# Two heads' scores on the row halves of TensorE, and values with scores in one run per block

## The chip, the cores and the metric

The kernel runs on one core of a Trainium2 chip. The metric is the device time of one execution in microseconds (us), lower is better. The engines are named as in the profile: PE (TensorE's products) and PEld (its weight loads), DVE (VectorE), ACT (ScalarE), POOL (GpSimd) and SP (SyncE, here only a queue of transfers).

## The reference

One layer of a decoder with three parallel groups of heads, for a new sequence of 4096 positions (the prompt) and for 8 x 8 single positions against a cache (the sample batch). Width 1024.

```python
def _layer(x, conv_buf, buf_k, buf_v, mem_k, mem_v, g_pre, g_post, w_in, conv_w, sink, w_out, prompt):
    h = _rmsnorm(x, g_pre)
    z = h @ w_in
    cb, cc, ch, cg, q, k, v, ag, mq, mg = _split_cols(z)
    u = cc * ch
    up = jnp.concatenate([conv_buf, u], axis=1)
    conv = conv_w[0] * up[:, 0:t] + conv_w[1] * up[:, 1:t + 1] + conv_w[2] * up[:, 2:t + 2]
    out_a = jax.nn.silu(cg) * cb * conv
    ...
    o_b = _window_prompt(q, k, v, sink_g)        # 8 heads of 64, 2 kv heads, window 128, one sink logit per head
    out_b = jax.nn.silu(ag) * o_b
    o_c = _mem_attend(mq.reshape(n, t, MEM_HEADS, HEAD_DIM), mem_k, mem_v)   # 4 heads of 64, 256 memory tokens
    out_c = jax.nn.silu(mg) * o_c
    y = jnp.concatenate([out_a, out_b, out_c], axis=-1) @ w_out
    return x + _rmsnorm(y, g_post), new_conv, new_k, new_v
```

Everything is float32. The softmax of the window takes the sink logit into its sum and its maximum. Outputs are y for prompt and sample batch and the new caches.

## The kernel before, in words

The first part, to about 952 us, is the input projection (products `c`, line L359). It leaves queries, keys, values and gates in DRAM (`qd`, `vd`, `md`). In its last third `third_jobs` weaves in the attention of chunk 0 and the scores of group 2.

The second part is the attention of the rest with the output projection. The prompt has 16 chunks of 256 positions (`CT`), each of two groups of 128 queries, so 32 groups; output block b is the 128 rows of group b. The blocks run in the order 0 to 30, 32 (the sample batch), 31. `Block.run` makes a block in two halves `y_0` and `y_1` of 512 columns, each 24 products of 128 x 512 (L1434): 8 steps k, and for each three products of high and low parts (`mh`, `ml`, which `split` makes on ACT and DVE). After each half DVE multiplies by the norm's weight into `yn` (L1441) and ACT squares with a row sum (L1442). After `y_1` DVE adds the sums (`yst`, L1447), POOL raises them to the power -1/2 (L1448), and DVE makes the residual sum `xr` (L1452), which is stored.

`events_of(i)` hangs the attention of later groups into block i, at (p, k): half p, ahead of step k. From block 2 on these are: at (0,4) `group_run`, the values of group i+2 with their gates (L1099, L1155) and the transposes of group i+3 (L1197, L1126); at (0,6), (1,0), (1,2) and (1,4) the four pieces of the scores of group i+4; at (1,0) also the split of block i+1. Loads of later chunks and the sample batch's stages hang in the same way. A scheduler orders each engine's instructions from this program; the engines then work through their orders.

A group's scores take eight window heads (`ws`, L1175) and four cross heads (`xs`, L1112). Queries lie with their high part on one half of the 128 rows and their low part on the other. Keys lie twice, with high parts (then low parts) on both halves, so two products of 128 rows and 256 columns per head sum all four combinations of parts. A piece of window scores is emptied from PSUM by an ACT copy of the own block's half (L1177) and a DVE copy_predicated of the earlier half (L1178), after which maximum, exps and scaling work in SBUF on four heads at a time. Cross scores are read from PSUM by maximum and exp. The transposed window weights are masked on POOL into `wpv` and `wpt` (L1204, L1207).

PSUM in this part has four banks in rotation for scores and transposes (tag `s`), two for y (tag `z`), and two for values (`pv`).

Of the kernel before, what the change touches and what calls it, by code (L numbers as in the profile page):

```python
# [51 lines left out]
def hybrid_layer(ctx: ExitStack, tc: tile.TileContext, a: dict):  # L52
# [664 lines left out]
    def third_start():  # L717
        keep = right.enter_context(tc.tile_pool(name="memkv", bufs=1, side="right"))
        third["mk"] = keep.tile([P, 2, 4, 256], F32R, name="mk")
# [64 lines left out]
    def mem_keys():  # L784
        mk, keys = third["mk"], third.pop("keys")
        t = third["ps"].tile([P, 512], F32, tag="m", name="mkt").rearrange("p (j m k) -> p j m k", j=2, m=2)
        for m in range(2):
            for j in range(2):
                TE.transpose(t[:, j, m, :], keys[:, m, j * P : (j + 1) * P], ident)
        for hh in range(2):  # L790
            src = t[hh * 64 : hh * 64 + 64].rearrange("p j m k -> p j (m k)")
            hi = mk[hh * 64 : hh * 64 + 64, 0, hh:4:2, :]
            for half in (hh, 1 - hh):
                r = slice(half * 64, half * 64 + 64)
                S.copy(mk[r, 0, hh:4:2, :], src)
                V.tensor_tensor(mk[r, 1, hh:4:2, :], src, f(hi), op=ALU.subtract)

    def third_jobs(b, p):
# [19 lines left out]
        if n > 13 and third["chunk"]:  # L818
            jobs.append(third["chunk"].pop(0))
        elif n > 13 and len(chunks) == 1:  # L820
            jobs.append(lambda: chunk_load(1))
        elif n > 13 and early[0] < 4 and n >= 38:
            jobs.append(lambda u=early[0]: scores(2, u))
            early[0] += 1
# [4 lines left out]
    def first_chunk():  # L829

        mem_stack.close()
        third["work"] = right.enter_context(tc.tile_pool(name="work", bufs=5, side="right"))
        chunk_load(0)
        chunk = chunks[0]
        chunk.load_mix()
        third["chunk"] = pieces = [lambda: chunk.values(None)]
        for left, right_, both in chunk.pairs():
            pieces += [lambda u=u: next(u, None) for _ in range(2) for u in (left, right_)] + [both]
# [141 lines left out]
    def open_attention():  # L980

        nonlocal ps, mixp, wp, xp, vp, bp, bq, yp
# [4 lines left out]
        ps = {tag: ctx.enter_context(tc.tile_pool(name=f"ps{tag}", bufs=bufs, space=bass.MemoryType.PSUM))  # L987
              for tag, bufs in (("s", 4), ("z", 2), ("pv", 1))}
        ps["t"] = ps["s"]
# [4 lines left out]
        xp = att.enter_context(tc.tile_pool(name="xp", bufs=2))  # L994
# [3 lines left out]
    ps = mixp = wp = xp = vp = bp = bq = yp = None  # L998
    att = ctx.enter_context(ExitStack())

    def psum(tag, name):
# [7 lines left out]
    def work(pool, shape, tag, name, **kw):  # L1009

        if ps is None or tag in ("sm", "p"):
            return third["work"].tile(shape, F32, tag="u", name=name)
        return pool.tile(shape, F32, tag=tag, name=name, **kw)

    def both_values(o, left, right):

        n = len(left)
        for i in range(n):
            for half, steps in enumerate((left, right)):
                v, p = steps[i]  # L1020
                cs = slice(64 * half, 64 * half + 64)
                TE.matmul(o[cs], v[:, cs], p, start=i == 0, stop=i == n - 1, tile_position=(0, 64 * half))  # L1022

    class Chunk:
# [10 lines left out]
        def load_keys(self):  # L1035
            c, t0 = self.c, self.t0

            self.kst = self.pool().tile([P, 4, P + CT], F32R, tag="k", name=f"kst{c}")
# [7 lines left out]
            self.vT = self.pool().tile([P, CT], F32, tag="vT", name=f"vT{c}")  # L1046
            DMA.dma_start(self.vT, vd[:, self.ts])

        def load_queries(self):

            self.q = self.pool(True).tile([P, 12, CT], F32R, tag="q", name=f"q{self.c}")
            for part in range(2):
                for hh in range(2):
                    half = hh if part == 0 else 1 - hh
                    G.dma_start(self.q[half * 64 : half * 64 + 64, hh::2, :],  # L1055
                                  qd[part, 1:7, hh * 64 : hh * 64 + 64, self.ts].rearrange("j p n -> p j n"))

        def load_mix(self):

            if self.c % 3 == 0:  # L1060
                self.mix = place.rearrange("p a k n -> p (a k n)")[:, : KT * CT].rearrange("p (k n) -> p k n", k=KT)
            else:
                self.mix = (yp if self.c % 3 == 2 else mixp).tile([P, KT, CT], F32, tag="mix", name=f"mix{self.c}", bufs=1)
            DMA.dma_start(self.mix, md[:, :, self.ts].rearrange("k p n -> p k n"))

        def values(self, vt_prev, pv=None):

            self.vts = [vt_prev]
            ts = [psum("t", f"vtp{self.c}_{i}")[:, 0:P] if pv is None else pv[:, 1, 256 + P * i : 256 + P * i + P] for i in range(2)]
# [10 lines left out]
        def pairs(self):  # L1080
            w, x = [self.window_pair(i) for i in range(2)], [self.cross_pair(i) for i in range(2)]
            return [w[0], x[0], w[1], x[1]]

        def group(self, i):

            return Group(self.window_pair(i), self.cross_pair(i))

        def cross_pair(self, j):

            pts = [[], []]  # L1090

            def both(pv=None):
                o = psum("pv", f"xo{self.c}_{j}")[:, :CT] if pv is None else pv[:, 0, 256 : 256 + CT]
                both_values(o, *([(third["mv"][:, kt, j * P : (j + 1) * P], pts[hh][kt]) for kt in range(2)]
                                 for hh in range(2)))

                def gate():
                    g = self.mix[:, 2 + j, :]
                    V.tensor_tensor(g, g, o, op=ALU.mult)  # L1099
                return gate if pv is not None else gate()  # L1100

            return *(self.cross_unit(2 * j + hh, pts[hh]) for hh in range(2)), both

        def cross_unit(self, h, pts):
            c, nb = self.c, CT // P
            q = self.q[:, h]
            p = work(xp, [P, nb, 256], "p", f"xp{c}_{h}")
            mx, nm, den, rd = (tiny.tile([P, 4], F32, tag=n, name=f"x{n}{c}_{h}") for n in ("mx", "nm", "den", "rd"))
            s = psum("s", f"xs{c}_{h}").rearrange("p (b k) -> p b k", b=nb)
            for i in range(nb):  # L1110
                for part in range(2):
                    TE.matmul(s[:, i, :], q[:, i * P : i * P + P], third["mk"][:, part, h, :], start=part == 0, stop=part == 1)  # L1112
            V.tensor_reduce(mx[:, :nb], s, axis=AX.X, op=ALU.max)
            V.tensor_scalar(nm[:, :nb], mx[:, :nb], -SCALE, None, op0=ALU.mult)  # L1114
            for i in range(nb):
                S.activation(p[:, i, :], s[:, i, :], AF.Exp, bias=nm[:, i : i + 1], scale=SCALE, accum_out=den[:, i : i + 1])  # L1116
            V.reciprocal(rd[:, :nb], den[:, :nb])  # L1117
            for i in range(nb):

                G.tensor_scalar(p[:, i, :], p[:, i, :], rd[:, i : i + 1], 0.5, op0=ALU.mult, op1=ALU.mult)  # L1120
            yield 1
            pt = work(xp, [P, 2, CT], "xpt", f"xpt{c}_{h}")
            t = psum("t", f"xt{c}_{h}").rearrange("p (k n) -> p k n", k=2)
            for kt in range(2):
                for i in range(nb):
                    TE.transpose(t[:, kt, i * P : (i + 1) * P], p[:, i, kt * P : (kt + 1) * P], ident)  # L1126
                pts.append(pt[:, kt])
            (S.copy if h % 2 else V.tensor_copy)(pt, t)


        def window_pair(self, i):

            steps = [[], []]

            def both_halves(pv):
                o = pv[:, :, :256].rearrange("p a (h q) -> p a h q", h=4)
                for n in range(2):  # L1140
                    for kvh in range(2):
                        cs = slice(64 * kvh, 64 * kvh + 64)
                        v, p3 = steps[kvh][n]
                        TE.matmul(o[cs, n], v[:, cs], p3[:, :, 64 * n : 64 * n + 64], start=True, stop=False,  # L1144
                                  tile_position=(0, 64 * kvh))
                for n in range(2):
                    for kvh in range(2):
                        cs, rs = slice(64 * kvh, 64 * kvh + 64), slice(64 - 64 * n, 128 - 64 * n)
                        v, p3 = steps[kvh][n]
                        TE.matmul(o[cs, 1 - n], v[rs, cs], p3[rs, :, 64 - 64 * n : 128 - 64 * n], start=False, stop=True,  # L1150
                                  tile_position=(64 - 64 * n, 64 * kvh))

                def gate():
# [477 lines left out]
```

## Time and profile before

| | |
|---|---|
| runs, median (lowest to highest) | 1551.85 us (1550.77 to 1553.34), 3 runs |
| the profiled execution, its own time | 1557.0 us |
| its span | 1555.2 us |
| granted TensorE clock over the span | 0.998 |
| PE busy in the span | 1535.2 us |
| DVE, ACT, POOL busy | 1155.1, 788.9, 377.8 us |

The profile is of one execution, and its times are in microseconds from the start of the span. A row of the timeline has the start, the length, engine, line, operation and tiles; "x8" says how many instructions were put together; brackets at its end tell how long the engine idled before it and what released it. A row of the chain of waits has start, length and the engine and line that the path runs through. A row of a stretch has its ends, its length, the busy time of PE, PEld, DVE, ACT and POOL (with instructions), the granted clock, the DMA share and GB/s.

### The profile page before, as it was taken

Reading aid. Unit: us, or ns where it says so; the run is one execution under the profiler, and the core shown is the slowest. Engines: PE = TensorE matmul, PEld = TensorE weight load, DVE = VectorE, ACT = ScalarE, POOL = GpSimd, SP = SyncE. Lnnn points to the kernel's source line nnn. Section 1 sums busy time; section 2 is a strip of 40 time slices with the busy share of each in tenths; the row PEclk is TensorE's granted clock in tenths of the full one; section 3 lists DMA queues with packets and bytes.
Section 4 is the critical chain, followed back from the end, with each engine's and each line's share of the span. In section 5 each row is a group of like instructions: output and inputs, shape, how many; then the busy total and the mean of one; then the engine's idle time right before and its main releaser. Section 6 shows DMA issues by size and latency. Waiting matters only on the chain.

```text
span 1555.2 us, 30088 instructions
## 1 busy us (share of the span) xinstructions
PE 1535.2 (99%) x11341; PEld 1405.0 (90%) x11341; DVE 1155.1 (74%) x2045; ACT 788.9 (51%) x1999; POOL 377.8 (24%) x602
## 2 busy tenths in 40 slices
PE   9989999999999999999999999999999999999998
PEld 9989999999999999999999998788888788888776
DVE  5769888898988777896687678666666666666653
ACT  6776666475322222344455446555565555565532
POOL 0222333211400000000001202544444444444310
PEclk9999999999999999999999999999999999999999
DMA  9979999878755333569666959986766666666432
GB/s 251 164 239 221 285 287 266 258 240 291 205 178 178 124 116 120 195 207 323 227 221 191 279 211 291 266 164 155 159 147 146 146 158 151 160 148 154 143 125 68
DMA packets 175110, 305.59 MB, mean 196 GB/s; under 512 B 31093, under 2 KB 104821, under 8 KB 174933
## 3 DMA queue, kind: packets, MB, share of 16 engines
q1 hardware_dynamic: 128069, 226.69, 47.3%
q0 software_dynamic: 46176, 75.92, 23.5%
q8 instruction: 90, 1.47, 0.4%
q10 hardware_dynamic: 720, 1.05, 0.2%
q14 instruction: 55, 0.45, 0.1%
HBM read 196.54 MB, written 108.05 MB: 196 GB/s over the span
## 4 chain that ended last, share of the span: by engine, by line
PE 81%; DMA 7%; DVE 5%; issue 3%; ACT 2%; POOL 1%; SPq 0%; ACTq 0%; DVEq 0%; POOLq 0%
PE c L359 42%; PE y L1434 23%; PE ws L1175 4%; PE xs L1112 2%; PE pv L1022 2%; PE wt L1197 2%; PE xt L1126 2%; PE pv L1144 2%; DMA nat<-in_x_p 1%; PE pv L1150 1%; DMA x_0B<-in_xt 1%; DMA x_7T<-hd_T 1%; PE mem_acc L775 1%; DMA vT<-vd 1%; DMA wr_2A<-in_w_in 1%
## 5 line engine op out<-in xcount | busy, mean ns | idle before, releaser
L1434 PE MATMUL y<-wo,mh 128*128 128x512 f32 (+1 forms) x1040 | 347.0, 392 | 0.0
L366 DVE TENSOR_TENSOR z<-c,z 128x520 f32<-128x520 f32 (+1 forms) x308 | 195.0, 645 | 93.9 <-PE c L359 92.7
L1434 PEld LDWEIGHTS y<-wo,mh 128*128 128x128 f32 x1040 | 194.7, 188 | 38.6 <-issue 2.8
L1434 PE MATMUL y<-wo,ml 128*128 128x512 f32 (+1 forms) x520 | 202.2, 389 | 0.0
L1188 ACT ACTIVATE sm<-sm,wnm 128x128 f32<-128x128 f32 x256 | 99.4, 389 | 76.9 <-DVE wnm L1182 76.9
L1120 POOL TENSOR_SCALAR xp<-xp,xrd 128x256 f32<-128x256 f32 x128 | 60.5, 485 | 265.0 <-DVE xrd L1117 265.0
L1434 PEld LDWEIGHTS y<-wo,ml 128*128 128x128 f32 x520 | 97.9, 188 | 14.2
L1177 ACT COPY sm<-ws 128x256 f32<-128x256 f32 x128 | 46.3, 369 | 66.6 <-PE ws L1175 63.3
L1175 PEld LDWEIGHTS ws<-kst,q 128*128 128x128 f32 x512 | 69.3, 191 | 5.8 <-ACT wpt L1199 1.2
L1441 DVE TENSOR_TENSOR yn<-y,gpost 128x512 f32<-128x512 f32 (+1 forms) x66 | 45.1, 683 | 37.6 <-PE y L1434 35.3
L1175 PE MATMUL ws<-kst,q 128*128 128x256 f32 x512 | 71.9, 283 | 0.8 <-ACT wpt L1199 0.8
L1178 DVE COPY_PREDICATED sm<-wmask,ws 128x256 f32<-128x256 uint8 x124 | 54.1, 442 | 18.1 <-ACT sm L1177 16.7
L1207 POOL TENSOR_SCALAR_AFFINE_SELECT wpt<-wpt 128x512 f32<-128x512 f32 x64 | 55.4, 893 | 45.7 <-ACT wpt L1199 45.4
L1452 DVE SCALAR_TENSOR_TENSOR xr<-yn,yst,xr 128x1024 f32<-128x1024 f32 (+2 forms) x34 | 42.7, 1258 | 30.0 <-POOL yst L1448 30.0
L734 POOL MEMSET negs<- 128x1 f32 x1 | 0.1, 98 | 264.6 <-PE c L359 264.6
L1116 ACT ACTIVATE xp<-xs,xnm 128x256 f32<-128x256 f32 x128 | 58.1, 461 | 3.9 <-DVE xnm L1114 3.7
L1055 POOL DMA_DIRECT2D q<-qd x64 | 42.8, 679 | 65.2 <-DMA qd<-zh 49.3
L1199 ACT COPY wpt<-wt 128x512 f32<-128x512 f32 x64 | 34.7, 588 | 44.6 <-PE wt L1197 28.0
L1204 POOL TENSOR_SCALAR_AFFINE_SELECT wpv<-wpt 128x512 f32<-128x512 f32 x62 | 39.6, 669 | 51.5 <-ACT wpt L1199 51.5
L368 ACT COPY z<-c 128x520 f32<-128x520 f32 (+1 forms) x44 | 24.4, 554 | 51.2 <-PE c L359 48.5
L1044 POOL DMA_DIRECT2D kst<-qd x64 | 38.7, 624 | 47.4 <-PE ws L1175 23.8
L1442 ACT ACTIVATE y<-y 128x512 f32<-128x512 f32 (+1 forms) x66 | 38.4, 582 | 22.6 <-DVE yn L1441 22.4
(962 smaller groups left out, 5119.3 us busy)
## 6 DMA issues: line engine op xcount, KB each, us to landing
q<-qd POOLq DMA_DIRECT2D x64, 384.0 KB, 7.6
xr<-in_x_p SPq DMA_DIRECT2D x32, 512.0 KB
nat<-in_x_p SPq DMA_DIRECT2D x39, 416.0 KB
o_yp<-xr SPq DMA_DIRECT2D x31, 512.0 KB
md<-th POOLq DMA_DIRECT2D x48, 260.0 KB, 6.3
qd<-zh SPq DMA_DIRECT2D x48, 260.0 KB
qd<-z SPq DMA_DIRECT2D x48, 260.0 KB
kst<-qd POOLq DMA_DIRECT2D x60, 192.0 KB, 3.6
```

The costliest lines, as they stand in the source:

```text
L359: TE.matmul(bank[:, :HW], l, r, start=first and i == 0, stop=last and i == 3 * KH - 1)
L366: add = lambda dst, other: V.tensor_tensor(dst, c, other, op=ALU.add)
L1055: G.dma_start(self.q[half * 64 : half * 64 + 64, hh::2, :], qd[part, 1:7, hh * 64 : hh * 64 + 64, self.ts].rearrange("j p n -> p j n"))
L1116: S.activation(p[:, i, :], s[:, i, :], AF.Exp, bias=nm[:, i : i + 1], scale=SCALE, accum_out=den[:, i : i + 1])
L1120: G.tensor_scalar(p[:, i, :], p[:, i, :], rd[:, i : i + 1], 0.5, op0=ALU.mult, op1=ALU.mult)
L1175: TE.matmul(s3[:, hh, :], self.q[:, 4 + 2 * (2 * half + hh) + kvh, i * P : i * P + P], self.kst[:, 2 * kvh + part, i * P : i * P + 2 * P], ...
L1177: S.copy(sm[:, 2 * half : 2 * half + 2, :], s3[:, :, P : 2 * P])
L1178: V.copy_predicated(sm[:, 2 * half : 2 * half + 2, :], third["wmask"], third["negs"].unsqueeze(2).to_broadcast([P, 2, P]) if first else s3 ...
L1188: S.activation(sm[:, hh, :], sm[:, hh, :], AF.Exp, bias=nm[:, hh : hh + 1], scale=SCALE, accum_out=den[:, hh : hh + 1])
L1207: G.affine_select(p3, p3, pattern=[[0, 4], [1, P]], compare_op=ALU.is_ge, fill=0.0, base=0, channel_multiplier=-1)
L1434: TE.matmul(acc, self.hl[l][:, k], wo[k][c0 // 512][:, r, c0 % 512 : c0 % 512 + c1 - c0], start=j == 0, stop=j == passes * KT - 1)
L1441: V.tensor_tensor(yn[:m, c0:c1], acc[:m], gpost[:m, c0:c1], op=ALU.mult)
```

## The change

A group's scores now use tiles of 64 rows. Two heads lie on the two row halves of the array, each with its own PSUM bank, and three products per head (high by high, low by high, high by low) take the place of the four combinations. So a group takes 36 products of 64 rows, in 18 pairs. Keys and queries are loaded once and not twice.

Values of group i+1 and then all scores of group i+3 stand at (0,0) of block i in one run, whose products are held in the program's order (`tiled`). The transposes of group i+2 stand at (1,0), the split of block i+1 at (1,3).

PSUM has six single banks b0 to b5 with fixed users, beside `pv`: window scores in 0 to 3, cross scores in 4 and 5, `y_0` in 0, `y_1` in 5, transposes of window weights in 1 and 2, of cross weights in 3 and 4. The window softmax of all eight heads is done at once. The sample batch's stages are hung at other places and banks. Shared work buffers are 3 of 1024 columns instead of 5 smaller ones.

```diff
-        if tag == "pv":
-
-            return ps[tag].tile([P, 2, 512], F32, tag=tag, name=name)[:, 0]
-        return ps[tag].tile([P, 512], F32, tag="s" if tag == "t" else tag, name=name)
+        return ps["b"].tile([P, 512], F32, tag=f"b{bank}", name=name)
...
+    def tiled(o, w, x, **kw):
+
+        ins = TE.matmul(o, w, x, **kw)
+        if run_open[0] and ps is not None:
+            tc.keep_in_program_order(ins)
+        run_open[0] = True
...
-            for kvh in range(2):
-                for half in range(2):
-                    G.dma_start(self.kst[half * 64 : half * 64 + 64, 2 * kvh : 2 * kvh + 2, lo:],
-                                  qd[:, 0, kvh * 64 : kvh * 64 + 64, t0 - P + lo : t0 + CT].rearrange("a p n -> p a n"))
+            G.dma_start(self.kst[:, :, lo:], qd[:, 0, :, t0 - P + lo : t0 + CT].rearrange("a p n -> p a n"))
...
+        def scores(self):
+            self.open_scores(0)
+            self.open_scores(3)
+            bands = [psum(n, f"ws{self.b}_{n}").rearrange("p (h k) -> p h k", h=2) for n in range(4)]
+            cross = [psum(4 + hh, f"xs{self.b}_{hh}").rearrange("p (j k) -> p j k", j=2) for hh in range(2)]
+            self.bands(bands[:2], 0)
+            self.crosses(cross)
+            self.bands(bands[2:], 1)
+            self.band_softmax()
+
+        def both_rows(self, outs, q, k):
+
+            for n, (qp, kp) in enumerate(((0, 0), (1, 0), (0, 1))):
+                for u in range(2):
+                    r = slice(64 * u, 64 * u + 64)
+                    tiled(outs[u], q[r, qp], k[r, kp], start=n == 0, stop=n == 2, tile_position=(64 * u, 0))
...
+        def band_out(self, s3, half, kvh):
+            to = self.sm[:, 4 * kvh + 2 * half : 4 * kvh + 2 * half + 2, :]
+            S.copy(to, s3[:, :, P : 2 * P])
+            V.copy_predicated(to, third["wmask"], third["negs"].unsqueeze(2).to_broadcast([P, 2, P]) if self.b == 0 else s3[:, :, 0:P])
...
+    def values_and_scores(i):
+
+        run_open[0] = False
+        if 2 <= i + 1 < 2 * NCH:
+            groups.pop(i + 1).values()
+        if i + 3 < 2 * NCH:
+            groups[i + 3] = Group(chunks[(i + 3) // 2], (i + 3) % 2)
+            groups[i + 3].scores()
...
-                acc = psum("z", f"y{b}_{p}")[:, : c1 - c0]
+                acc = psum((0, 5, 1)[p], f"y{b}_{p}")[:, : c1 - c0]
...
+        at(0, 0, values_and_scores, i)
         if i + 2 < len(blocks):
-            at(0, 0 if i != 26 else 1, blocks[i + 2].load)
...
-            at(0, 4, group_run, i + 2, i + 3)
-            at(0, 6, scores, i + 4, 0)
-            at(1, 0, scores, i + 4, 1)
-            at(1, 0, split)
-            at(1, 2, scores, i + 4, 2)
-            at(1, 4, scores, i + 4, 3)
+            at(0, 0, blocks[i + 2].load)
...
+        at(1, 0, transposes, i)
+        if i + 1 < len(blocks) and blocks[i + 1].b != 32:
+            at(1, 3, blocks[i + 1].split)
```

More of the change, by code (lines that the diff above doesn't have):

```diff
@@ L789, in mem_keys @@
                 TE.transpose(t[:, j, m, :], keys[:, m, j * P : (j + 1) * P], ident)
[L790 to L796, printed above, removed]
+        src = t.rearrange("p j m k -> p j (m k)")
+        S.copy(mk[:, 0], src)
+        V.tensor_tensor(mk[:, 1], src, f(mk[:, 0]), op=ALU.subtract)
     def third_jobs(b, p):
@@ L831, in first_chunk @@
         mem_stack.close()
-        third["work"] = right.enter_context(tc.tile_pool(name="work", bufs=5, side="right"))
+        third["work"] = right.enter_context(tc.tile_pool(name="work", bufs=3, side="right"))
         chunk_load(0)
         chunk = chunks[0]
+        chunk.load_values()
         chunk.load_mix()
-        third["chunk"] = pieces = [lambda: chunk.values(None)]
-        for left, right_, both in chunk.pairs():
-            pieces += [lambda u=u: next(u, None) for _ in range(2) for u in (left, right_)] + [both]
+        third["chunk"] = [lambda: chunk.values(None)]
+        for i in range(2):
+            pair = Group(chunk, i)
+            third["chunk"] += [lambda pair=pair, n=n, fn=fn: fn(pair, n) for fn, ns in (
+                (Group.early_scores, (0, 1, 2)), (Group.early_transposes, (0, 1)), (Group.early_values, (1,)),
+                (Group.early_scores, (3,)), (Group.early_transposes, (2, 3)), (Group.early_values, (3,))) for n in ns]
     sums_at = {(0, 3 + i): pair for i, pair in enumerate(PHASES[1])}
@@ L1078, in values @@
                 self.vts.append(vt)
[L1080 to L1102, printed above, removed]
@@ L1124, in cross_unit @@
-            for kt in range(2):
[L1125 to L1153, printed above, removed]
-                    g = self.mix[:, 4:8, i * P : i * P + P].rearrange("p h (a q) -> p a h q", a=2)
-                    V.tensor_tensor(g, g, o, op=ALU.mult)
-                return gate
-            def both():
-                o = psum("pv", f"wo{self.c}_{i}")
-                both_values(o, *steps)
-                gate = self.mix[:, 4:8, i * P : i * P + P]
-                V.tensor_tensor(gate, gate, o.rearrange("p (h q) -> p h q", h=4), op=ALU.mult)
-            return *(self.window_unit(i, kvh, steps[kvh]) for kvh in range(2)), both if self.c == 0 else both_halves
@@ L1210, in hybrid_layer, with early_transposes @@
-    class Group:
-        def __init__(self, window, cross):
-            self.units, self.both = [*window[:2], *cross[:2]], (cross[2], window[2])
-        def scores(self, n):
-            next(self.units[n])
-        def transposes(self):
-            for unit in self.units:
-                next(unit, None)
-    groups = {}
-    def scores(g, n):
-        if g < 2 * NCH:
-            if n == 0:
-                groups[g] = chunks[g // 2].group(g % 2)
-            groups[g].scores(n)
-    def group_run(values, transposes):
-        gates, c = (), transposes // 2
-        fresh = transposes % 2 == 0 and c < NCH
-        if values < 2 * NCH or fresh:
-            pv = ps["pv"].tile([P, 2, 512], F32, tag="pv", name=f"pv{transposes}")
-        if 2 <= values < 2 * NCH:
-            gates = [both(pv) for both in groups.pop(values).both]
-        if fresh:
-            chunks[c].values(chunks[c - 1].vts[2], pv)
-        for gate in gates:
-            gate()
-        if transposes < 2 * NCH:
-            groups[transposes].transposes()
+        def early_transposes(self, n):
+            if n == 0:
+                pt = work(f"wpt{self.b}").rearrange("p (u n) -> p u n", u=2)
+                pv = work(f"wpv{self.b}").rearrange("p (u n) -> p u n", u=2) if self.b else None
+                for u in range(2):
+                    self.pt[u], self.pv[u] = pt[:, u], pv[:, u] if self.b else None
+            if n == 2:
+                xpt = work(f"xpt{self.b}").rearrange("p (u n) -> p u n", u=2)
+                for u in range(2):
+                    self.xpt[u] = xpt[:, u]
+            if n < 2:
+                self.band_transposes(n, psum(0, f"wt{self.b}_{n}"))
+            else:
+                self.cross_transposes(n - 2, psum(0, f"xt{self.b}_{n}"))
@@ new lines, in cross_transposes, with cross_values @@
+        def cross_transposes(self, u, t):
+            t3 = t.rearrange("p (k n) -> p k n", k=2)
+            for kt in range(2):
+                for j in range(2):
+                    TE.transpose(t3[:, kt, j * P : (j + 1) * P], self.p[:, u, j, kt * P : (kt + 1) * P], ident)
+            (S.copy if u else V.tensor_copy)(self.xpt[u], t)
+        def cross_values(self, o):
+            c = self.chunk
+            for j in range(2):
+                both_values(o[:, j * P : j * P + P], *([(third["mv"][:, kt, j * P : (j + 1) * P],
+                                                         self.xpt[hh][:, CT * kt + P * j : CT * kt + P * j + P]) for kt in range(2)]
+                                                       for hh in range(2)))
+            g = c.mix[:, 2:4, self.i * P : self.i * P + P]
+            V.tensor_tensor(g, g, o.rearrange("p (j n) -> p j n", j=2), op=ALU.mult)
@@ new lines, in early_values @@
+        def early_values(self, n):
+            c = self.chunk
+            if n == 3:
+                self.cross_values(psum(0, f"xo{self.b}")[:, :CT])
+                return
+            o = psum(0, f"wo{self.b}")
+            both_values(o, *([(v, p[u]) for v, p in zip(c.vts[self.i : self.i + 2], (self.pv, self.pt)) if p[u] is not None]
+                             for u in range(2)))
+            g = c.mix[:, 4:8, self.i * P : self.i * P + P]
+            V.tensor_tensor(g, g, o.rearrange("p (h q) -> p h q", h=4), op=ALU.mult)
@@ L1408, in split @@
             if b == 32:
-                hi = mixp.tile([P, KT, CT], F32R, tag="mix", name="mh_s", bufs=1)[:, :, :P]
+                hi = third["work"].tile([P, KT, P], F32R, tag="u", name="mh_s")
                 S.copy(hi[:, :, 0:NS], mix_s)
@@ L1460, in hybrid_layer @@
     chunk_load(2)
+    chunks[2].load_values()
     blocks[0].load()
```

274 lines of the change are left out of this document (144 added, 130 removed).

## The prediction

> **What bounds the kernel now.** I read the page's busy shares first, then the chain of work that ended last, then one stretch of the output stage (twenty whole blocks) by engine and by instruction.
>
> ```profile
> span 1555.2 us, 30088 instructions
> PE 1535.2 (99%) x11341; PEld 1405.0 (90%) x11341; DVE 1155.1 (74%) x2045; ACT 788.9 (51%) x1999; POOL 377.8 (24%) x602
> PE 81%; DMA 7%; DVE 5%; issue 3%; ACT 2%; POOL 1%; SPq 0%; ACTq 0%; DVEq 0%; POOLq 0%
> 1088.96:1456.16 367.20, 367.20 (x2262) 297.64 (x2261) 247.76 (x601) 212.32 (x780) 163.02 (x266) 1.00 0.67 154
> ```
>
> The last row gives a stretch, its length and the busy time of PE, weight load, DVE, ACT and POOL. PE is busy for all of the 367.20 us: 18.36 us per block, at full clock, with nobody else near it. The chain through one block, in order of time:
>
> ```profile
> 1015.52 5.46 PE y L1434 x24
> ...
> 1107.43 5.46 PE y L1434 x24
> 1112.89 1.01 PE pv L1022 x8
> 1113.90 0.86 PE pv L1144 x8
> 1114.77 0.59 PE pv L1150 x8
> 1115.36 1.02 PE wt L1197 x8
> 1116.38 0.87 PE xt L1126 x8
> ...
> 1118.65 0.96 PE ws L1175 x8
> ...
> 1123.34 0.47 PE xs L1112 x4
> ...
> 1125.68 5.46 PE y L1434 x24
> ...
> 1133.62 0.37 PE pv L1071 x2
> ```
>
> It never leaves PE. Of 18.36 us a block spends 2 x 5.46 = 10.92 on the projection, 2.46 on values, 1.89 on transposes (and 0.37 in every second block), 2 x 0.96 + 2 x 0.47 = 2.86 on scores. Two x24 pieces lie 18.25 apart. No product waits for another engine, because scores come in four pieces among the y products with four banks to land in, and y has two banks of its own.
>
> **What the change takes from PE.** Scores go from 24 products of 128 rows to 36 of 64 rows, run as 18 pairs. A product of 256 columns takes 0.96 / 8 = 0.12 us, so 18 x 0.12 = 2.16 if a pair takes the time of one: 0.70 less per block. That pairs overlap the trace shows with other tiles of 64 rows, which begin 0.01 us apart:
>
> ```profile
> 1114.70 0.43 PE L1150 MATMUL pv<-wpv,vt 64*64 64x256 f32 x2
> 1114.71 0.43 PE L1150 MATMUL pv<-wpt,vt 64*64 64x256 f32 x2
> ```
>
> Each change of tile shape costs: the first eight value products take 1.01, the next eight of that shape 0.86, so 0.15 to 0.2. One boundary is added per block (0.2). PE work per block falls by 0.5, to about 17.9. If PE stayed the bound, 29 full blocks would save some 13 us.
>
> **What it puts in the way.** At (0,0) of block i now stand the values of group i+1 and all scores of group i+3, in one run. From the end of y_1's last product this run takes 0.15 + 0.86 (cross values) + 0.86 + 0.59 + 0.2 + 2.16 + 0.2 = 5.0 us. Then comes y_0, and y_0 now writes bank 0, the bank of ws_0, the first score of the same run. So y_0's first product waits until DVE's copy_predicated has emptied ws_0. In the instruction order of the changed kernel DVE does the following between y_1 and that copy: yn of y_1, the cross gate, yst, xr, the gate of pv, ml, and only then the copy for ws_0. These lines of before give their prices, and what they wait for:
>
> ```profile
> 1110.21 0.69 DVE L1441 TENSOR_TENSOR yn<-y,gpost 128x512 f32<-128x512 f32 x1 [0.88 <-PE y L1434]
> 1112.80 0.21 DVE L1447 TENSOR_SCALAR yst<-yst 128x1 f32<-128x1 f32 x1 [0.44 <-ACT y L1442]
> 1113.74 1.26 DVE L1417 TENSOR_TENSOR ml<-mix,mh 128x1024 fp32r<-128x1024 f32 x1 [0.72 <-ACT mh L1416]
> 1115.47 1.28 DVE L1452 SCALAR_TENSOR_TENSOR xr<-yn,yst,xr 128x1024 f32<-128x1024 f32 x1 [0.47 <-POOL yst L1448]
> 1116.67 0.41 DVE L1099 TENSOR_TENSOR mix<-mix,pv 128x256 f32<-128x256 f32 x1
> 1117.00 0.68 DVE L1155 TENSOR_TENSOR mix<-mix,pv 128x512 f32<-128x512 f32 x1
> ...
> 1119.56 0.93 DVE L1178 COPY_PREDICATED sm<-wmask,ws 128x256 f32<-128x256 uint8 x2 [1.28 <-ACT sm L1177]
> ...
> 1132.74 1.28 DVE L1452 SCALAR_TENSOR_TENSOR xr<-yn,yst,xr 128x1024 f32<-128x1024 f32 x1 [1.48 <-POOL yst L1448]
> ...
> 1136.57 1.49 DVE L1417 TENSOR_TENSOR ml<-mix,mh 128x1024 fp32r<-128x1024 f32 x1 [0.45 <-ACT mh L1416]
> ```
>
> ```profile
> 1112.06 0.59 ACT L1442 ACTIVATE y<-y 128x512 f32<-128x512 f32 x1
> 1112.57 0.20 ACT L1442 ACTIVATION_READ_ACCUMULATOR y<-y 128x1 f32 x1
> 1112.66 1.05 ACT L1416 CAST mh<-mix 128x1024 fp32r<-128x1024 f32 x1
> ```
>
> ```profile
> 1113.90 1.53 POOL L1448 TENSOR_TENSOR yst<-yst,mhalf 128x1 f32<-128x1 f32 x1
> 1132.15 0.56 POOL L1448 TENSOR_TENSOR yst<-yst,mhalf 128x1 f32<-128x1 f32 x1
> ```
>
> Count from the end of y_1's last product slot; a first reader starts 0.2 later (estimate: 12 of the 24 products after 1107.43 end at 1110.16, yn starts at 1110.21, and I add 0.15 for the end of a pipelined product). yn 0.20 to 0.89. Square and its accumulator read, 1112.06 to 1112.77, so 0.71: done at 1.64. yst 0.21: 1.89. POOL's power 0.56: 2.5. xr 1.28: 3.8. Gate of pv 0.68, starting just before xr's record ends: 4.4. ACT casts mh from that gate's result, 1.05: 5.5. ml 1.26: 6.8. Copy of ws_0, half of 0.93 less overlap: 7.15. y_0 starts at 7.2. PE could have started it at 5.0, so it stands for about 2.2 us in every block. ACT's own copy of ws_0 sits behind mh, ready at about 6, and is covered by ml.
>
> The power has two prices. It took 1.53 where ml was running on DVE (1113.74 to 1115.00) and 0.56 where DVE stood idle for 1.48 ahead of xr. In the new order DVE has nothing left to do while it waits for the power, so I take 0.56. The Trainium skill ("Trainium Architecture — The Big Picture", What this means for kernel authors) says that DVE and GpSimd share one port pair under an exclusive lock. The two rows agree with it, and by that rule the short price holds in the new order as well.
>
> That DVE does not step over a waiting instruction shows at 1115.47: it idled 0.47 for POOL's result while the cross gate, whose products ended at 1113.90, ran only behind it. So the copy of ws_0 cannot pass xr or ml.
>
> The bounds of this chain: with a power of 1.53 or ml at 1.49 it ends at 8.2 to 8.4, and with a pipelined start of yn at 0.05 at 7.0. The stall is 2.0 to 3.4.
>
> **What else moves, at nothing.** y_1 takes bank 5, whose cross scores are read by exps and a maximum while y_0's 5.46 us run. Transposes at (1,0) go to banks 1 to 4, which are emptied during y_0. The masks that the values need come from POOL:
>
> ```profile
> L1207 POOL TENSOR_SCALAR_AFFINE_SELECT wpt<-wpt 128x512 f32<-128x512 f32 x64 | 55.4, 893 | 45.7 <-ACT wpt L1199 45.4
> ...
> L1204 POOL TENSOR_SCALAR_AFFINE_SELECT wpv<-wpt 128x512 f32<-128x512 f32 x62 | 39.6, 669 | 51.5 <-ACT wpt L1199 51.5
> ```
>
> Two of each are 3.1 us, and y_1's 5.46 lie between the transposes and the next values. kst and q come in 3 transfers per chunk instead of 8, all on POOL's queue, which shortens it; the load of values moves by some products on SP's queue, a block or more ahead of its use. The split, now at (1,3), serves the next block, with a whole y_0 in hand. Twice as many cross value products of half the columns keep the columns. If one of these covers is gone it costs up to about 1 us a block (estimate: 3.1 of masks behind late transposes, less the 2.2 of stall that hides part of it); that is in the range.
>
> **The sum.** Period after: 7.2 + 5.46 + (0.87 + 0.87 + 0.19) + 5.46 = 20.05, against 18.36: +1.69.
> - Start of the stage. Before, block 2 ends in the middle of the x24 piece at 1015.52, so at about 1018.2. After, y_0 of block 0 can start when DVE has emptied ws_0, behind its last conversions of the projection:
>
> ```profile
> 955.72 1.91 DVE L402 TENSOR_TENSOR z<-z,zh 128x520 fp32r<-128x520 f32 x3
> ...
> 958.15 0.77 DVE L1178 COPY_PREDICATED sm<-wmask,ws 128x256 f32<-128x256 uint8 x2
> ```
>
> that is at 958. Three blocks of 5.46 + 1.9 + 5.46 = 12.8 and two stretches of 7.2 between them end at 1010.9: -7. These blocks carry less, since groups run one block later than before.
> - Blocks 3 to 25: 23 x 1.69 = +38.9.
> - Blocks 26 to 30. Before: 2 x 18.36 + (18.36 - 2.86) + (10.92 + 2.46) + 10.92 = 76.5. After, one block later with each kind of work: 3 x 20.05 + 15.3 + 13.4 = 88.8: +12.2. The sample batch's products are the same in both.
> - Early attention inside the projection: 9 score pieces with up to 0.4 of changed shape each, +3.6, less three groups' 0.70: +1.4.
>
> In all +45.5 on the profiled execution's 1557.0 us: 1602.5. That execution lies 5 us above the median of the runs, 1551.85, so on the median's footing the time is **1597**.
>
> **Rivals.** Main case, 0.75: as above; own range 1575 to 1628.
>
> PE stays the bound, 0.12: DVE's chain ends before PE's run, at under 5 us instead of 7.2, for instance because instructions overlap on ACT and DVE more than single rows show. Break-even with before is a start of y_0 at 5.5, so 1.7 us must be missing from the sum of eight rows. For it: before has DVE idle a third of the time. Against it: every step waits for the one before. Stage periods 17.9, no stall: start -11, blocks -11, end +6, early +1.4, about -15: **1537**.
>
> The long chain, 0.08: power and ml at their long prices, y_0 at 8.4, stall 3.4, period 21.25. Then -5 + 23 x 2.89 + 16 + 1.4 = +79: 1631. It has a second step. Before shows a PE gap that was followed by half clock, and one that was not:
>
> ```profile
> PE rows_y L300 <- DVE mix_s L291: 4.5, 2, 4.2
> PE wt L1197 <- ACT y L1442: 1.8, 1, 1.8
> ...
> 90.37:93.78 3.41, 3.41 (x15) 3.13 (x14) 1.39 (x3) 2.13 (x5) 0.00 (x0) 0.50 0.95 227
> ```
>
> After the 4.2 us gap the granted clock is 0.50 for 3.41 us, which costs 1.7 us; after the 1.8 us gap it stayed. Stalls between the two would cost up to 1.7 x 28 = 48 more: 1679. The Trainium skill ("TensorE: Matmul & The Clock Gate", Why this matters for your kernels) puts the limit at about 3 us without matmuls. By that rule the main case's 2.2 keeps the clock and this rival loses it.
>
> Row halves that do not overlap, 0.05: 36 x 0.12 = 4.3 us of scores, a run of 7.2 us, just as late as the copy of ws_0: +0.2 a block, 1602. The change would then not do what it says, and time would hardly tell.
>
> **How the numbers follow.** The likeliest case gives 1597. Faster by over 0.2% (3 us, about what the runs of this kernel can tell apart) is the second case alone, 0.12; within it 0.01, for a chain that ends near break-even; slower 0.87. The range leaves out the 1537 and the clock's loss: 1565 to 1632, the lower end at a start of y_0 near 6.2 (29 x 1.0 less).
>
> **What would show it.** Right: in PE's waits, y's line waiting for DVE's sm some 28 times at 2.0 to 2.5 us; the chain passing through DVE, ACT and POOL once a block; y_0 starting 7.2 us after y_1's end, a period near 20.05; 18 pairs of scores in 2.2 us; clock 1.00 in the stage; PE's share falling to about 95%. Wrong: no gap ahead of y_0, periods under 18.4, or the wait ending on something else than the copy of ws_0.

## The result, and the profile after

The changed kernel takes 1606.58 us (median of 4 runs, 1604.41 to 1607.5) against 1551.6 us (1550.77 to 1553.34): a ratio of 1.0351, 95% interval 1.0333 to 1.0369. It is slower by 55 us. Its profiled execution took 1605.98 us, with a span of 1604.3 us and a granted clock of 0.996. Below are the head of its page with the shares of its chain, and then the same stretch of 23 whole blocks (3 to 25) in both kernels, before's first:

```profile
span 1604.3 us, 30846 instructions
PE 1529.8 (95%) x11981; PEld 1399.3 (87%) x11981; DVE 1128.4 (70%) x1850; ACT 777.4 (48%) x1964; POOL 324.2 (20%) x522
PE 64%; DVE 14%; issue 8%; ACT 7%; POOL 3%; DMA 3%; SPq 0%; POOLq 0%; ACTq 0%; DVEq 0%
```

```profile
1018.10:1440.49 422.39, 422.39 (x2602) 342.39 (x2600) 285.21 (x690) 244.42 (x900) 191.21 (x309) 1.00 0.68 153
```

```profile
1019.92:1483.05 463.13, 416.74 (x3059) 335.46 (x3059) 268.39 (x553) 235.97 (x873) 149.42 (x245) 1.00 0.43 128
```

PE's busy time in the 23 blocks fell from 422.39 to 416.74, while the stretch grew to 463.13: PE now stands for 2.0 us in each block, and all engines do less per microsecond. What it waits for:

```profile
PE y L1458 <- DVE sm L1142: 42.7, 29, 3.3
PE pv L1017 <- DVE mix L1218: 8.6, 14, 0.6
PE pv L1017 <- DVE place L1218: 8.6, 14, 0.6
```

Columns are total, number and longest. y waits for the copy of ws_0 in 29 blocks, and the products of the values wait 0.62 for the cross gate in 28. Next comes one block boundary in the timelines of PE, DVE, ACT and POOL. Its first row is y_1's last product; such products follow each other every 0.23, so its slot ends at 1093.29:

```profile
1093.06 0.39 PE L1458 MATMUL y<-wo,mh 128*128 128x512 f32 x1
1093.38 1.09 PE L1017 MATMUL pv<-xpt,mv 128*64 128x128 f32 x16
1095.09 0.65 PE L1017 MATMUL pv<-wpv,vt 128*64 128x256 f32 x4 [0.62 <-DVE place L1218]
...
1096.69 0.97 PE L1017 MATMUL ws<-kst,q 64*128 64x256 f32 x12
1097.50 0.88 PE L1017 MATMUL xs<-mk,q 64*128 64x256 f32 x12
1098.22 0.88 PE L1017 MATMUL ws<-kst,q 64*128 64x256 f32 x12
1100.52 0.50 PE L1458 MATMUL y<-wo,mh 128*128 128x512 f32 x1 [1.42 <-DVE sm L1142]
```

```profile
1093.48 0.69 DVE L1465 TENSOR_TENSOR yn<-y,gpost 128x512 f32<-128x512 f32 x1 [3.80 <-PE y L1458]
1094.52 0.42 DVE L1218 TENSOR_TENSOR place<-place,pv 128x256 f32<-128x256 f32 x1 [0.34 <-PE pv L1017]
1094.99 0.21 DVE L1471 TENSOR_SCALAR yst<-yst 128x1 f32<-128x1 f32 x1
1095.89 1.28 DVE L1476 SCALAR_TENSOR_TENSOR xr<-yn,yst,xr 128x1024 f32<-128x1024 f32 x1 [0.69 <-POOL yst L1472]
1097.09 0.68 DVE L1250 TENSOR_TENSOR place<-place,pv 128x512 f32<-128x512 f32 x1
1098.89 1.23 DVE L1441 TENSOR_TENSOR ml<-place,mh 128x1024 fp32r<-128x1024 f32 x1 [1.11 <-ACT mh L1440]
1100.03 0.77 DVE L1142 COPY_PREDICATED sm<-wmask,ws 128x256 f32<-128x256 uint8 x2
```

```profile
1097.81 1.05 ACT L1440 CAST mh<-place 128x1024 fp32r<-128x1024 f32 x1 [2.85 <-DVE place L1250]
```

```profile
1095.29 0.57 POOL L1472 TENSOR_TENSOR yst<-yst,mhalf 128x1 f32<-128x1 f32 x1 [3.95 <-DVE yst L1471]
```

Read DVE's rows from the top: yn, the cross gate, xr and ml each begin on another engine's result, named in the brackets, and y_0 begins at 1100.52, 7.23 after y_1's end. The scores run as 18 pairs in 2.25 us while this chain is still under way.

### The profile page after: what moved, and what is told of

Same layout as the page of the kernel before. It is cut to its first block, busy times and chain, and to the rows that moved or that the text cites. A ratio compares the mean times of both kernels' runs of the same rounds, so it can differ in the third digit from the quotient of the medians.

```text
span 1604.3 us, 30846 instructions
## 1 busy us (share of the span) xinstructions
PE 1529.8 (95%) x11981; PEld 1399.3 (87%) x11981; DVE 1128.4 (70%) x1850; ACT 777.4 (48%) x1964; POOL 324.2 (20%) x522
## 4 chain that ended last, share of the span: by engine, by line
PE 64%; DVE 14%; issue 8%; ACT 7%; POOL 3%; DMA 3%; SPq 0%; POOLq 0%; ACTq 0%; DVEq 0%
PE c L359 47%; PE y L1458 12%; ACT sm L1153 3%; DVE xr L1476 2%; DVE ml L1441 2%; ACT mh L1440 2%; DVE sm L1142 2%; DVE wmx L1148 1%; POOL wpt L1202 1%; DVE xmx L1161 1%; POOL yst L1472 1%; PE xt L1208 1%; PE wt L1195 1%; PE mem_acc L775 1%; ACT y L1466 1%
## 5 line engine op out<-in xcount | busy, mean ns | idle before, releaser
L1458 PE MATMUL y<-wo,mh 128*128 128x512 f32 (+1 forms) x1040 | 338.9, 396 | 42.7 <-DVE sm L1142 42.7
L1200 POOL TENSOR_SCALAR_AFFINE_SELECT wpv<-wpt 128x512 f32<-128x512 f32 x62 | 51.8, 855 | 98.7 <-ACT wpt L1196 98.7
L1017 PEld LDWEIGHTS ws<-kst,q 64*128 64x128 f32 x768 | 50.2, 187 | 12.1 <-issue 10.8
L1017 PE MATMUL ws<-kst,q 64*128 64x256 f32 x768 | 60.0, 288 | 0.4 <-DVE z L366 0.4
L1017 PE MATMUL pv<-wpv,vt 128*64 128x256 f32 (+1 forms) x240 | 39.1, 400 | 17.2 <-DVE mix L1218 8.6
L1202 POOL TENSOR_SCALAR_AFFINE_SELECT wpt<-wpt 128x512 f32<-128x512 f32 x64 | 40.6, 653 | 50.7 <-ACT wpt L1196 50.4
L1142 DVE COPY_PREDICATED sm<-wmask,ws 128x256 f32<-128x256 uint8 x124 | 49.9, 441 | 0.0
L1472 POOL TENSOR_TENSOR yst<-yst,mhalf 128x1 f32<-128x1 f32 (+1 forms) x33 | 18.4, 557 | 148.0 <-DVE yst L1471 148.0
L1153 ACT ACTIVATION_READ_ACCUMULATOR sm<-sm,wnm 128x1 f32 x256 | 47.9, 187 | 0.0
L400 ACT CAST zh<-z 128x520 fp32r<-128x520 f32 x56 | 33.4, 624 | 29.2 <-DVE z L366 26.5
```

The lines of the kernel that those rows point to most:

```text
L1017: ins = TE.matmul(o, w, x, **kw)
L1142: V.copy_predicated(to, third["wmask"], third["negs"].unsqueeze(2).to_broadcast([P, 2, P]) if self.b == 0 else s3[:, :, 0:P])
L1153: S.activation(sm[:, h, :], sm[:, h, :], AF.Exp, bias=nm[:, h : h + 1], scale=SCALE, accum_out=den[:, h : h + 1])
L1200: G.affine_select(self.pv[u].rearrange("p (h q) -> p h q", h=4), p3, pattern=[[0, 4], [-1, P]], compare_op=ALU.is_gt, fill=0.0, base=0, ch ...
L1202: G.affine_select(p3, p3, pattern=[[0, 4], [1, P]], compare_op=ALU.is_ge, fill=0.0, base=0, channel_multiplier=-1)
L1458: TE.matmul(acc, self.hl[l][:, k], wo[k][c0 // 512][:, r, c0 % 512 : c0 % 512 + c1 - c0], start=j == 0, stop=j == passes * KT - 1)
```

## The experiments

Each ratio below is to runs of the kernel before on the same chip. The experiments ran on different chips, so two of them are compared by their ratios, times 1551.6 us; where the plain medians say something else, both are given. The first three edits take one link of the chain each.

**The split kept in its place.**

```diff
-            S.copy(hi, src)
-            V.tensor_tensor(lo, src, f(hi), op=ALU.subtract)
+            pin(S.copy(hi, src))          # pin = tc.keep_in_program_order in this stage
+            pin(V.tensor_tensor(lo, src, f(hi), op=ALU.subtract))
```

> The changed kernel with one edit: mh and ml of the next block keep their place in the program (at (1,3), inside y_1) instead of standing ahead of the copy of ws_0. Theory (DVE's chain ahead of the copy of ws_0 sets the start of y_0): the chain loses mh 1.05 and ml 1.23, the copy ends some 4.8 us after y_1, earlier than PE's own run (5.65 in the changed kernel, a 0.62 wait for the cross gate included), so y_0 starts at about 5.65 instead of 7.23: 29 x 1.55 = 45 us less, about 1561, with no wait of y for the copy left. Rival (the price lies in the run itself, the row halves or the added changes of shape, and the wait only shows it): PE loses nothing, 1600 to 1607.

Measured: 1568.89, ratio 1.0095 (1.0067 to 1.0123). By the ratios some 40 of the 55 us lost come back by moving two instructions, neither of which PE needs there. The wait of y for the copy is gone but for the first block, a block takes 429.43 / 23 = 18.67, and the 0.6 us for the cross gate stays. The theory's 1561 is 8 low, and the rival's 1600 is refuted.

```profile
PE pv L1017 <- DVE place L1218: 8.8, 14, 0.8
...
PE y L1459 <- DVE sm L1142: 3.3, 1, 3.3
...
1020.84:1450.27 429.43, 415.28 (x3061) 335.29 (x3059) 287.95 (x553) 237.50 (x873) 154.90 (x240) 1.00 0.48 138
```

**The residual sum made later.**

```diff
+            def finish(pin=lambda ins: ins):
+                ...                        # xr and its store, as before
+        at(0, 1, lambda: blocks[i - 1].finish(tc.keep_in_program_order))
```

> The changed kernel with one edit: the residual sum xr of block i is made and stored inside y_0 of block i+1, so DVE no longer waits for POOL's power ahead of the gates. Theory: the gate of pv then waits for PE's values (end at 3.46) instead of xr (end at 3.88), so the chain shortens by some 0.35 only, not by xr's 1.28: 29 x 0.35 = 10 us less, about 1596. Rival (each link of DVE counts with its whole length): 1.28 + 0.57 a block, about 1553. Rival (the run itself): no change.

Measured: 1601.41, ratio 1.0308 (1.0285 to 1.0331). Taking 1.28 us of xr and the wait for POOL out of DVE's way is worth only some 7 us by the ratios, since the gate of pv behind it then waits for the products of the values, as DVE's row shows. A link is worth the distance to the next thing that is late, not its length.

```profile
1156.11 0.69 DVE L1250 TENSOR_TENSOR mix<-mix,pv 128x512 f32<-128x512 f32 x1 [1.63 <-PE pv L1017]
```

**The cross gate behind the values.**

```diff
-            self.cross_values(pv[:, 0, 256 : 256 + CT])
+            gate = self.cross_values(pv[:, 0, 256 : 256 + CT])
...
+            gate()                         # behind the products of the values
```

> The changed kernel with one edit: the cross gate stands behind the products of the values, so these no longer wait 0.62 for it. DVE then makes it behind xr. Theory: PE's run ends 0.62 earlier, which is worth nothing, and the chain is longer by the cross gate's 0.35: 29 x 0.35 = 10 us more, about 1616. Rival (PE's run sets the start of y_0): 29 x 0.62 = 18 less, about 1588.

Measured: 1637.8, ratio 1.0515 (1.0468 to 1.0562), so 25 us more than the changed kernel by the ratios (31 by the medians), though PE's wait for the gate is gone. The sign is the theory's and the size is more than twice its 10. Two blocks of it in PE's timeline, and two stretches of the first:

```profile
1199.05 0.50 PE L1459 MATMUL y<-wo,mh 128*128 128x512 f32 x1 [2.90 <-DVE sm L1142]
...
1202.34 0.63 PE L1459 MATMUL y<-wo,ml 128*128 128x512 f32 x1
...
1243.21 0.50 PE L1459 MATMUL y<-wo,mh 128*128 128x512 f32 x1 [2.62 <-DVE sm L1142]
```

```profile
1199.75:1200.40 0.65, 0.65 (x5) 0.52 (x4) 0.65 (x2) 0.00 (x0) 0.00 (x0) 1.00 0.87 353
1200.40:1203.80 3.40, 3.40 (x10) 2.63 (x9) 2.55 (x10) 2.89 (x14) 0.97 (x3) 0.50 0.03 12
```

PE now stands once for 2.6 to 2.9 us instead of twice for 0.62 and 1.42. In the first of these blocks the clock then falls to 0.50 for 3.40 us (products of 0.63 instead of 0.39), 1.35 us after PE has started again; in the second it does not. It is not the 0.28 between these two gaps that decides: the block at 1154.52 lost the clock behind a gap of 2.62 as well. From the first product of y_0 to that of y_1 it takes 8.7 to 9.1 us in 11 of the blocks 3 to 25 and 7.2 to 7.5 in the other 12; all gaps but two are 2.61 to 2.63 long, on both sides. What decides is not shown. The 11 cost 11 x 1.6 = 18 us; without them a block takes (489.55 - 18) / 23 = 20.5, which is the 0.35 more that was expected.

```profile
1028.33:1517.88 489.55, 428.77 (x3059) 346.31 (x3059) 270.42 (x553) 237.22 (x873) 160.03 (x246) 0.96 0.40 121
```

**More work in the gap.** Is it the gap that takes the clock?

```diff
-            for n, (qp, kp) in enumerate(((0, 0), (1, 0), (0, 1))):
+            for n, (qp, kp) in [*enumerate(((0, 0), (1, 0), (0, 1)))] * (1 if ps is None else 2):
```

> e3_gates_behind with every score product of the run made twice. Theory (in e3 PE stands for 2.8 us in one piece, after which the clock is granted at half for 3.4 us): the run ends at 7.2 instead of 5.03, PE stands for 0.6 us only, the clock stays, and a block takes 7.8 + 12.85 = 20.65 instead of 22.25. More work makes it faster: 29 x 1.6 = 46 us less than e3's 1638, about 1592 (1585 to 1612). Rival (the half clock comes from something else than the gap): as e3 or slower, 1638 to 1660.

Measured: 1619.19, ratio 1.0419 (1.0388 to 1.0449): 15 us less by the ratios (19 by the medians) than without the extra products. In the 23 blocks the clock is 1.00, PE waits 0.5 per block, and a block takes 472.05 / 23 = 20.52, where 20.65 was expected. So the gap took the clock. The total expected, 1585 to 1612, was too low, because 22.25 for a block of e3 is the length of blocks that lost the clock (those from 1176.54 to 1221.05); over 23 blocks it was 21.28.

```profile
PE y L1459 <- DVE sm L1142: 16.7, 29, 2.5
...
1021.15:1493.20 472.05, 461.15 (x3886) 383.63 (x3886) 273.10 (x553) 235.07 (x873) 151.00 (x240) 1.00 0.44 126
```

**The same extra work in the changed kernel.** This is the same edit with the cross gate left in its place.

> The changed kernel with every score product of the run made twice (the second time over the first), 2.16 us more work for PE in each of 29 blocks. Theory: 1.4 of it lies under the wait for the copy of ws_0, the run ends at 7.8 instead of 5.65, y_0 starts at 7.8 instead of 7.23: 29 x 0.57 = 17 us more, about 1624. Rival (PE's work sets the time): 29 x 2.16 = 63 more, about 1669.

Measured: 1629.96, ratio 1.0482 (1.0448 to 1.0516). 63 us of added products cost 20 by the ratios, and y_0 no longer waits for the copy except in two blocks. So some two thirds of the added work are hidden under the chain, and a shorter run alone would not have shown in the time.

```profile
PE y L1458 <- DVE sm L1142: 1.8, 2, 1.5
```

**The three products alone, in the old schedule.** The cross gate stands behind the values and the split at (1,1); groups still run one block later than before.

```diff
+        for tag, bufs in (("s", 4), ("z", 2)):
+            ps[tag] = ...                  # banks as before
-        at(0, 0, values_and_scores, i)
-        at(1, 0, transposes, i)
+        at(0, 4, values_and_scores, i)     # values alone
+        at(0, 4, transposes, i)
+        at(0, 6, piece, i, 0)
+        at(1, 0, piece, i, 1)
+        at(1, 0, piece, i, 2)              # the window's softmax
...
+        at(1, 3, piece, i, 3)
```

> The three products on row halves alone, in the schedule of before: values and transposes at (0,4), the scores in three pieces among the products of y, four banks in rotation for them and two of its own for y, the gates behind the values. Theory (the price is the run and the shared bank, not the three products): no wait of y; a block costs PE 18.36 - 0.70 + 3 x 2 changes of shape at 0.2 = 18.9, groups still one block later than before: about 1565 (1550 to 1575). If a change of shape costs nothing, 1535 to 1545. Rival (64-row tiles are what costs): 1600 or more.

Measured: 1569.91, ratio 1.0103 (1.0081 to 1.0126). PE never waits in the 23 blocks, and a block takes 432.68 / 23 = 18.81. The first row below is the 23 blocks; the chain of one block shows why three products do not pay in this form:

```profile
1009.11:1441.79 432.68, 432.68 (x3059) 330.57 (x3058) 282.09 (x553) 237.45 (x874) 158.91 (x240) 1.00 0.50 140
...
1148.24 1.40 PE y L1467 x6
1149.64 0.90 PE ws L1020 x12
1150.54 1.58 PE y L1467 x6
1152.12 0.91 PE ws L1020 x12
1153.03 2.28 PE y L1467 x9
```

12 score products take 0.72 inside a run (1097.50 to 1098.22 above); here they take 0.90 to 0.91, and the six y products behind them 1.58 instead of 1.40. Each piece pays about 0.19 on entering the tile shape and again on leaving it, 1.1 us a block against the 0.70 saved. So the run at one place has its reason.

**Two and three edits together.**

> The two edits of e1_split_late and e3_gates_behind together: mh and ml inside y_1, the cross gate behind the products of the values. Theory (y_0 starts when the later of PE's run and DVE's copy of ws_0 is done): the run without the wait for the gate ends at 5.03, the chain without mh and ml, but with the cross gate behind xr, at 5.2. A block takes 5.25 + 12.85 = 18.1 instead of e1's 18.65: 29 x 0.55 = 16 us less than e1's 1569, about 1553. Rival (edits do not add, since the cross gate behind xr cost 31 us alone): 1570 to 1600.

Measured: 1567.0, ratio 1.0082 (1.0055 to 1.0109): no gain over the split alone, where 1553 was expected. In DVE's timeline and in PE's:

```profile
1159.46 1.70 DVE L1443 TENSOR_TENSOR ml<-mix,mh 128x1024 fp32r<-128x1024 f32 x1 [1.64 <-ACT mh L1442]
1161.08 0.68 DVE L1467 TENSOR_TENSOR yn<-y,gpost 128x512 f32<-128x512 f32 x1
```

```profile
1166.10 0.50 PE L1460 MATMUL y<-wo,mh 128*128 128x512 f32 x1 [0.96 <-DVE sm L1142]
```

ml in y_1 runs beside POOL's masks, takes 1.70, and ends at 1161.16, one microsecond after y_1's last product slot (1160.15), so yn and all behind it start 0.7 late. So it is in every second block; in the others ml takes 1.43 and yn is some 0.4 late. The moved work pushed the chain from the other side. With xr moved as well there is room:

> All three edits together: mh and ml inside y_1, gates behind the values, xr inside the next y_0. Theory: the copy of ws_0 is done at 4.5, PE's run ends at 5.03 and sets the start of y_0, as PE's own work does in the kernel before: a block of 17.9, about 1547, 0.3% less than before. Rival (xr in front of yn of y_0, ml in y_1 and the rest of DVE's work now crowd and delay transposes or y_1): 1555 or more.

Measured: 1549.75 (10 runs), ratio 0.9972 (0.9956 to 0.9988): a little faster than before, and 59 us faster, by the ratios, than the change as it was made.

```profile
PE y L1460 <- DVE sm L1142: 3.2, 1, 3.2
...
1015.06:1431.44 416.38, 416.38 (x3061) 337.90 (x3059) 292.21 (x553) 237.40 (x873) 202.38 (x240) 1.00 0.49 144
```

PE is busy for the whole of the 23 blocks again, at 18.10 each instead of 18.36. That 0.26 is what the three products in one run are worth here, with the changes of shape that come with the run.

**The first block.** One wait of 3.2 us was left in that kernel, ahead of block 0, with a clock of 0.50 behind it.

```diff
+                acc = values_psum("y0_0")[:, 0, : c1 - c0] if b == 0 and p == 0 else ...
-        at(1, 0, transposes, i)
+        at(1, 0 if i else 3, transposes, i)
```

> e6_all with one more edit: y_0 of block 0 goes to the values' banks, which are free there, so it no longer waits 3.2 us for the copy of ws_0, and the first transposes stand at (1,3). Theory: the wait of 3.2 us and the half clock of some 3.4 us behind it (1.7) both go: 4.9 less than e6, about 1545. If the wait alone goes (the clock falls for another reason): 1546.5. Rival (the output weights, which DVE still prepares there, make y_0 wait just as long): 1550, as e6.

Measured: 1556.31 (12 runs), ratio 1.0004 (0.9989 to 1.0018): a miss, some 5 us slower by the ratios than without the edit. y_0 of block 0 does start earlier, with a wait of 1.0 for ml left in it. But yn, the first reader of y_0, then waits for a transfer. The transposes of the values use the lent banks and wait for ACT to square y_0, which stands behind the window's exps and with them behind yn on DVE:

```profile
974.22 0.69 DVE L1467 TENSOR_TENSOR yn<-y,gpost 128x512 f32<-128x512 f32 x1 [4.65 <-DMA qd<-z]
...
978.19 0.69 PE L1075 MATMUL vtp<-ident,vT 128*128 128x128 f32 x2 [4.35 <-ACT y L1468]
```

The gap also took the clock, which is 0.50 from 978.50 to 981.90. In the kernel without the edit yn starts 14.7 after the projection's last product, here 15.5: the transfer sets it, and starting y_0 earlier moved PE's wait behind it. Which transfer it is stays open: the profile names the one that came last, and yn also needs the norm's weights, whose load is issued at 962.32.

## Why the prediction was right

In the blocks the mechanism, its place and its size are those predicted; at the start of the stage the agreement is partly luck. y_0 starts 7.23 after y_1's end where 7.2 was worked out from rows of before, and a block takes 463.13 / 23 = 20.14 against 20.05. The three steps of the sum, from the profiled executions:

| | predicted | measured |
|---|---|---|
| up to block 3 (1018.10 before; 1019.92 - 7.23 after) | -5.6 | -5.4 |
| blocks 3 to 25 | +38.9 | +40.7 |
| blocks 26 to 30 | +12.2 | +13.8 |
| sum | +45.5 | +49.1, the difference of the spans |

The last row of them comes from these stretches, before's and after's:

```profile
1440.49:1530.15 89.66, 89.66 (x559) 68.02 (x557) 51.67 (x121) 38.99 (x129) 18.58 (x35) 1.00 0.35 121
```

```profile
1475.80:1579.26 103.46, 97.42 (x701) 73.62 (x701) 55.23 (x123) 44.55 (x151) 25.01 (x53) 1.00 0.33 114
```

The first row of the table agrees by luck as much as by working. Both traced executions stood once in the projection and then lost some time at a clock of 0.50: before 4.19 us at 89.95, the changed kernel 2.58 us at 375.59. Such waits come and go between executions: seven of the nine experiments' traces have one at the first of these places, of 1.80 to 4.65 us, and two have none. The projection's last product starts at 951.74 before and at 950.25 after, so 1.5 of the 5.4 come from there, and only 3.9 from the first three blocks, where the prediction had 7. What it left out is the half clock of the first block: behind a wait of 3.28 its y_0 took 8.17 us, against 5.60 in the block shown above. On the medians, 55.0 in all less 54.5 for blocks 3 to 30, the time up to block 3 hardly changed, by +0.5 and not by -5.6.

The predicted 1597 is 9.6 below 1606.58. 3.6 of that are the sum's. The larger part is the footing: the 5 us by which before's profiled execution lay above its median were taken off the result, but after's profiled execution lies at its own median, so they did not carry over. That these 5 us are before's long gap in the projection is likely, not shown: its other runs have no trace. It is the same 6 us by which the first row of the table misses on the medians.

Some terms held for other reasons than given. PE's stall was put in one place, 2.2 us ahead of y_0. It is 0.62 ahead of the values and 1.42 ahead of y_0: the products of the values wait for the cross gate, since it is made at once behind the cross products and reads the same tile. The prediction did not see this wait. Being under DVE's chain it changed no time. And PE's work fell by 0.26 us a block, not by 0.5, as the kernel with all three edits shows: in its chain the values take 2.65 where the prediction kept 2.46, and entering the scores and leaving them cost about 0.2 each, where it had counted 0.2 once. Both errors lay where nothing is paid.

The price of the power held: 0.57 in 1095.29's row, with DVE idle beside it. The lock on the port pair of which the Trainium skill speaks ("Trainium Architecture — The Big Picture", What this means for kernel authors) agrees with that, and with ml's 1.70 in e5, where it overlaps POOL's masks, against 1.23 here.

The rivals: that PE stays the bound is refuted by the waits and by e7, where doubling the scores cost a third of their time. The row halves overlap: pairs of the run take 0.72 / 6 = 0.12, the price of one product. The long chain did not come, but its second step is real, and nearer than thought. The prediction put the clock's loss at stalls somewhere between 1.8 and 4.2, and had the Trainium skill's limit ("TensorE: Matmul & The Clock Gate", Why this matters for your kernels) of about 3 us beside it. Gaps of 2.6 us took the clock in about half the cases in e3. In the projection shorter ones did too: behind gaps of 1.80 (e3), 2.10 (e2) and 2.15 (e5) the clock is 0.50 for some 3.4 us, while it stayed at 1.00 behind 1.78 (before) and 1.89 (e1). So no single length divides them in these traces, and the page's limit of about 3 us is too high for this case. The changed kernel's 2.0 us came in two parts, of at most 1.50 from the second block on, and kept the clock; e3, which seemed to free PE, made one longer gap of them.

Left open: what the early attention in the projection costs, since the waits there differ between the two executions by as much, and what decides whether a gap of 1.8 to 2.6 us takes the clock.

## What to carry to other kernels

When work is bundled into one run and its banks are shared with the main products, look in the order of the emptying engine at everything that stands ahead of the first bank's release: the bundle is only as early as that engine's queue. An instruction that nobody needs soon (here the split for the next block) can be the most expensive one in it, because here the scheduler placed it as soon as its inputs were there. Removing a link gives the distance to the next late thing, so links are tried together as well as alone, and after each move it is worth looking at what the moved work now stands ahead of.

## What the runs showed of the hardware that was not expected

- Gaps of PE of 2.6 us can halve the granted clock: in e3 it happened in 11 of 23 blocks with nearly equal gaps, for some 3.4 us of products each time, 1.6 us lost. Gaps of 0.62 and 1.42 with some 4.0 us of products between them did not in 28 blocks. Single gaps in the projection did at 1.80, 2.10 and 2.15, and did not at 1.78 and 1.89. The Trainium skill ("TensorE: Matmul & The Clock Gate", Part 1: The HAM clock gate) speaks of a window of activity that runs freely; that equal gaps end differently fits with it, but no run here measured its phase.
- Adding 2.2 us of useless products per block to e3 made it 15 to 19 us faster.
- Changing between 64-row and 128-row tiles costs PE about 0.19 us each way (e4: 12 score products 0.91 instead of 0.72, six y products behind them 1.58 instead of 1.40).
